# A two-layer hybrid decoder trunk: a changed order of work, u of the second layer handed over per 512 features, and a last normalisation without GpSimd

## The chip, the cores and the metric

The kernel runs on one core of one Trainium2 chip. The metric is the device time of one execution in microseconds; the figure of a kernel is the median of its runs. The core has five engines with a queue each: TensorE (PE in the profile, its weight loads PEld), VectorE (DVE), ScalarE (ACT), GpSimd (POOL) and SyncE (SP), which here issues almost all DMAs. An engine works through its queue in order, and waits at an instruction whose data is not there.

## The reference

Two layers, 256 rows of 1024 features, one batch. Each layer is:

```
mod = c @ w_ada + b_ada -> (shift, scale, gate)
u   = x * (1 + scale) + shift
h   = u @ w_in                      (one projection, columns split among groups)
o   = concat[DSA(4 heads), FoX(6 heads), NSA(6 heads)] * silu(g_path)
x   = LayerNorm(ALPHA * x + (1 + gate) * (o @ w_out)) * ln_g + ln_b
```

DSA is attention over the 64 best keys of each row, chosen by an indexer with 8 small heads. FoX is causal attention with a decay that is a running sum of log-sigmoids. NSA adds three branches: compressed keys, selected blocks and a window; at 256 rows the last two are both causal attention over all keys. The output is x after the second layer, in float32.

## The kernel before

**Products.** Each float32 operand of a projection is split in two: a rounded part (wh, uH, mH) and the rest (wl, uL, mL). A product is three matmuls in turn, rounded by rounded, rounded by rest, rest by rounded (`mm3`, L549 to L551). For a weight piece ACT makes wh (L516) and DVE wl (L534).

**Weights.** All weights are one stream of pieces of up to 128 x 1024 float32, 512 KB each, read in a fixed order (`stream_order`, L180) by SP into six raw buffers (L485). A raw buffer is free when DVE has made wl from it, or, for a piece of w_ada, when DVE has multiplied it with c and summed it up (`ada_gemv`, L583, one piece per 128 features and part). The order's parameters are `cord` (order of the four column chunks of layer 1), `tord0` and `tord1` (order of the 16 column tiles), `ada_at` and `adag_at` (behind which tile the pieces of w_ada come: the pair of a start and a step).

**Projections.** Four chunks, A to D, are projected with rows on the partitions: A holds the indexer, decay and NSA gates, B q and k of DSA, C keys of NSA, D queries of NSA; each also carries a part of the values. Layer 0 does all four chunks together, piece by piece. Layer 1 does them one after the other in the order `cord` (`proj_tok`, L1146); the first one takes rows 0 to 127 with its four pieces, then rows 128 to 255 with the same pieces. A unit is one piece of 256 features for one half of the rows, six matmuls. Then come 16 column tiles (`proj_col`, L1164): 0 and 1 are the compressed NSA keys and values, 2 to 7 keys and queries of the three FoX pairs (2 and 3 are pair 0, 4 and 5 pair 1, 6 and 7 pair 2), 8 to 15 the gate path, one per pair of heads (8 and 9 DSA, 10 to 12 NSA, 13 to 15 FoX).

**Attention.** Two heads make a pair (`attn_pair`, L713): scores in two PSUM banks (L722), row maximum on DVE (L677), exponential on ACT (L681), reciprocal sums on DVE (L667, L668), scaling on ACT (L694), transposes on PE (L704), copy on ACT (L708), product with the values on PE (L753), copy out of PSUM (L975). An NSA pair does this twice in one output bank and then waits for the compressed branch. The gate step (`out_gate`, L1123) takes one of four gate buffers, frees its PSUM bank once it has multiplied, waits for its head pair, and makes mH and mL.

**End of a layer.** The output projection is followed by `resid` (L1223): gate row times y (L1229), ALPHA x + that (L1232), statistics (L1234, L1245), then `rsqrt` (L1290): variance plus EPS on DVE (L1246), Ln and Exp on ACT (L1292, L1293), two ACT products that prepare a Newton step (L1294, L1295), and two DVE steps for it (L1297, L1298). After layer 0 x is normalised (L1263), PE transposes it (L1379, `next_u`), ACT makes u (L1389) and uH (L1403), and DVE uL (L1407, `u_block`), each for 512 features and 128 rows. The old layer's scale and shift go into the new layer's modulation; x itself gets them later (`affine`, L1420, four DVE operations L1430 per half of the rows). After layer 1 the rows 0 to 127 are normalised on ACT (L1281, `tail_first`) and get ln_g and ln_b on GpSimd (L1287, `tail_pool`); rows 128 to 255 get theirs on DVE (L1304, L1307, `tail`).

**What sets the order.** A planner (`Order`, L233) writes the queues out when the program is built. Each part of the work is a task that asks for an engine and states a cost, for buffers or PSUM banks, or for an event (`until`). The planner gives each engine the task that can start first, and among those that can start within 0.02 us of it (0.1 for a task of priority -2 or less) the one with the lowest priority number. The numbers stand in `PR` (L364), by layer where the name ends in 0 or 1: `nsa`, `dsa`, `fox` the pairs, `idx`, `topk`, `dec`, `cmp` the indexer, the selection, the decay and the compressed branch, `aff` the affine step, `ada` 6, the main stream 10. PSUM banks are given by class with a cap each: `acc` 4 of the 8 banks for projections, `o` 3 for outputs, `s` 2 for scores, `pt` 1 for transposes, `ms` 3. Events only shape the plan; on the chip an instruction waits for its data.

The event of the handover is set when both blocks of 512 features are there:

```
yield until(("ub", t, 0), ("ub", t, 1))     # next_u, L1381
od.set("u", 1, t)
...
yield until(("u", l, t), ("w", (c, l, q)))  # proj_tok, L1153
...
yield until(("u", 1, 0))                    # stream, L1435
```

Of the kernel before, what the change touches and what calls it, by code (L numbers as in the profile page):

```python
# [13 lines left out]
ALU = mybir.AluOpType  # L14
# [4 lines left out]
P = 128  # L19
# [341 lines left out]


RW = [6, 5]
PR = dict(zn='VV', upart=4, ul='VVVV', nrm='AAAA', cord='ABDC', t1q=0, cuts=(0, 512, 1024), oq=(0, 1, 2, 3), tord=(0, 1, 2, 3, 4, 5, 6, 7, 8, 9, 10, 11, 12, 13, 14, 15), gpp=(0, 1), res=-3.5, warm=10, tol=0.1, ada_at=(12, 0.25), adag_at=((0, 0.5), (11, 1)), ow=(512, 256), aff=0, tw=512, nact=((0, 0), (1, 0), (0, 1), (1, 1)), pro='', gp0=(0, 1), gp1=(0, 1), acc=4, s=2, pt=1, o=3, ms=3, side=8, topk=3, idx=2, dec=0.5, cmp=1.2, nsa=1.6, dsa=1.7, fox=1.8, gate=4, gate1=6, ada=6, main=10, ev=0, split=4, nahead=2, acc1=1.5, cmp1=3, dec0=1.45, nsa1=1.6, topk1=6, nsa0=1.3, dec1=0.5, idx1=0.3, tord1=(2, 3, 4, 5, 6, 7, 0, 1, 8, 9, 10, 11, 12, 13, 14, 15), dsa0=1.4, oq0=(1, 0, 2, 3), cmp0=1.2, fox1=1.5, dsa1=1.7, fox0=1.1, oq1=(1, 2, 3, 0), topk0=3, tord0=(0, 1, 2, 3, 4, 5, 6, 7, 8, 9, 10, 11, 12, 13, 14, 15), idx0=2, nrm1='AAAA', nrm0='AAAA', t1q0=0, t1q1=0)  # L364


@with_exitstack
def trunk(ctx: ExitStack, tc: tile.TileContext, xT, x, crow, wst, bcol, lnrow, pe_b, cst, cstb, out,
# [30 lines left out]
    def until(*names):  # L399
        return ("U", names)  # L400
# [14 lines left out]
    def small(shape, name, bufs=2, dt=F32, pool=None):  # L415
        return (pool or sm).tile(shape, dt, tag=name, name=nm(name), bufs=bufs)
# [350 lines left out]
    def layer(l, uH, uL):  # L767
# [378 lines left out]
        def proj_tok(c, t_outer=False):  # L1146
            n = len(CHUNKS[c])
            yield bank("acc", 2)
            accs = [ps(n) for _ in range(2)]
            units = [(t, q) for t in range(2) for q in range(4)] if t_outer else \  # L1150
                    [(t, q) for q in range(4) for t in range(2)]
            for t, q in units:
                yield until(("u", l, t), ("w", (c, l, q)))  # L1153
                yield ("P", rmm(n, 6))
                h, lo = piece((c, l, q), n)
                for k in (2 * q, 2 * q + 1):
                    ts = slice(t * P, (t + 1) * P)
                    mm3(accs[t], uH[:, k, ts], uL[:, k, ts], h[:, k % 2, :], lo[:, k % 2, :], k == 0, k == 7)
                if t == 1:
                    piece_done((c, l, q))  # L1160
                if q == 3:
                    od.spawn(EV[c](t, accs[t], "acc"), 0)
# [28 lines left out]
        if l == 0:  # L1191
            yield bank("abc", 8)
            accs = {c: [ps(len(CHUNKS[c])) for t in range(2)] for c in "ABCD"}
            for j in range(8):
                yield until(("uk", j))
                for grp in FIRST[j]:
                    key = (grp, l, j)
                    yield until(("w", key))
                    n = len(CHUNKS[grp[0]])
                    yield ("P", rmm(sum(len(CHUNKS[c]) for c in grp), 6))  # L1200
                    h, lo = ready[key]
                    for cc in grp:
                        cs = slice(0, n) if cc == grp[0] else slice(n, n + len(CHUNKS[cc]))
                        for t in range(2):
                            ts = slice(t * P, (t + 1) * P)
                            mm3(accs[cc][t], uH[:, j, ts], uL[:, j, ts], h[:, cs], lo[:, cs], j == 0, j == 7)
                    piece_done(key)
            od.set("u", 0, 0)
            od.set("u", 0, 1)
            for c in "ABCD":  # L1210
                for t in range(2):
                    od.spawn(EV[c](t, accs[c][t], "abc"), 0)
        else:
            for c in PR["cord"]:
                yield from proj_tok(c, t_outer=(c == PR["cord"][0]))
# [7 lines left out]
        def resid(t, o, w, acc):  # L1223
            yield until(("grow", l, o // 512))
            yield lock("t2k")
            xs = x_sb[:, t, o:o + w]
            yield ("V", cvec(w))
            tmp = buf("t2k", 512)[:, :w]
            V.tensor_tensor(tmp, acc, Gr[l][:, o:o + w], op=ALU.mult)  # L1229
            unbank("acc")  # L1230
            yield ("V", cvec(w, 2))
            V.scalar_tensor_tensor(xs, xs, ALPHA, tmp, op0=ALU.mult, op1=ALU.add)  # L1232
            for i in range(0, w, 256):
                V.bn_stats(stats[:, t, (o + i) // 256, :], xs[:, i:i + 256])  # L1234
            od.release("t2k")
            if o + w < D:
                return
            mv = small([P, 2], "mv", 2)
            ve = small([P, 1], "ve", 2)
            rs = small([P, 1], "rs", 2)  # L1240
            rm = small([P, 2], "rm", 2)
            tq = small([P, 1], "tq", 2)
            mu = mv[:, 0:1]
            yield ("V", 0.2)
            V.bn_aggr(mv, stats[:, t].rearrange("p n s -> p (n s)"))  # L1245
            V.tensor_scalar(ve, mv[:, 1:2], EPS, None, op0=ALU.add)  # L1246
            od.set("res", l, t)
            od.spawn(rsqrt(t, ve, rs, rm, tq), -3)
            if l + 1 < DEPTH:
                yield until(("rs", l, t))  # L1250
                if "A" in PR["zn"]:
                    nb = small([P, 1], "nb", 2)
                    yield ("V", 0.1)
                    V.scalar_tensor_tensor(nb, mu, -1.0, tq, op0=ALU.mult, op1=ALU.mult)
                od.spawn(next_u(l, t), -2)
                for q in range(2):
                    xs = x_sb[:, t, 512 * q:512 * q + 512]
                    if PR["zn"][q] == "A":
                        yield ("A", cact(512, 1))
                        A.activation(xs, xs, AF.Identity, bias=nb, scale=tq)  # L1260
                    else:
                        yield ("V", 0.12 + cfast(512))
                        V.tensor_scalar(xs, xs, mu, tq, op0=ALU.subtract, op1=ALU.mult)  # L1263
                    od.set("zn", t, q)
                od.spawn(affine(t), PR["aff"])
            elif t == 0:
                od.spawn(tail_first(mu, tq), 6)
            else:
                cuts = PR["cuts"]
                for i, (o0, o1) in enumerate(zip(cuts, cuts[1:])):  # L1270
                    od.spawn(tail(t, o0, o1, mu, tq, i), -2)

        def tail_first(mu, tq):
            nb = small([P, 1], "nb", 2)
            yield until(("rs", l, 0))
            yield ("V", 0.08)
            V.scalar_tensor_tensor(nb, mu, -1.0, tq, op0=ALU.mult, op1=ALU.mult)
            for h in range(2):
                xs = x_sb[:, 0, 512 * h:512 * h + 512]
                yield ("A", cact(512, 2))  # L1280
                A.activation(xs, xs, AF.Identity, bias=nb, scale=tq)  # L1281
                od.spawn(tail_pool(xs, h), 6)

        def tail_pool(xs, h):
            for i, op in enumerate((ALU.mult, ALU.add)):
                yield ("G", cpool(512))
                G.tensor_tensor(xs, xs, rows[l][i][:, 512 * h:512 * h + 512], op=op)  # L1287
            nc.sync.dma_start(out[:, 0, 512 * h:512 * h + 512], xs)

        def rsqrt(t, ve, rs, rm, tq):  # L1290
            yield ("A", 0.5)
            A.activation(rs, ve, AF.Ln)  # L1292
            A.activation(rs, rs, AF.Exp, scale=-0.5)  # L1293
            A.mul(rm[:, 0:1], rs, -0.5)  # L1294
            A.mul(rm[:, 1:2], rs, 1.5)  # L1295
            yield ("V", 0.54)
            V.scalar_tensor_tensor(tq, rs, rs, ve, op0=ALU.mult, op1=ALU.mult)  # L1297
            V.tensor_scalar(tq, tq, rm[:, 0:1], rm[:, 1:2], op0=ALU.mult, op1=ALU.add)  # L1298
            od.set("rs", l, t)

        def tail(t, o0, o1, mu, tq, i):
# [63 lines left out]
    def next_u(l, t):  # L1365
# [5 lines left out]
        for q in range(2):  # L1371
# [6 lines left out]
                j = 4 * q + i  # L1378
                T.transpose(pt[:, i, :], x_sb[:, t, P * j:P * j + P], ident)  # L1379
            od.spawn(u_block(q, pt, t), -2)  # L1380
        yield until(("ub", t, 0), ("ub", t, 1))  # L1381
        od.set("u", 1, t)

    def u_part(q, i, pt, u, t):
        j = 4 * q + i
# [9 lines left out]
    def u_block(q, pt, t):  # L1395
# [11 lines left out]
        (V if E == "V" else G).tensor_tensor(uL1[:, 4 * q:4 * q + 4, ts], u, uH1[:, 4 * q:4 * q + 4, ts].bitcast(F32), op=ALU.subtract)  # L1407
        od.release("t2k")
        od.set("ub", t, q)

    rows = {}

# [19 lines left out]

    def stream():
        yield from layer(0, uHs[0], uLs[0])
        yield until(("u", 1, 0))  # L1435
        yield from layer(1, uHs[1], uLs[1])

    u_tiles(0)
# [46 lines left out]
```

## Time and profile before

| | |
|---|---|
| median of 3 runs | 391.98 us (390.94 to 393.09) |
| the profiled execution | 391.34 us, of which its span 389.6 |
| mean granted clock of TensorE | 0.965 |
| PE busy | 352.2 us, 90% |
| DVE busy | 314.6 us, 81% |
| ACT busy | 252.6 us, 65% |
| POOL busy | 8.1 us, 2% |
| moved by DMA | 75.47 MB, mean 194 GB/s |

A row of a profile names engine, line, operation, the tiles it writes and reads, their shapes, and how many instructions were merged (x4). Times are microseconds; start times count from the span's start. L549 to L551, L516 and L534 are lines of helpers, so that the tiles tell what the row belongs to: wh,uH is an input projection, wh,mH an output projection. Tile b is any PSUM bank, q and f are attention operands, lnr rows of ln_g and ln_b, mv mean and variance. A busy PE may be one at half clock; the granted clock says so.

### The profile page before, as it was taken

What the parts mean: (1) busy time and instruction counts of PE and PEld (TensorE: products, weight loads), DVE (VectorE), ACT (ScalarE), POOL (GpSimd) and SP (SyncE); (2) the same over time, 40 slices, a digit from 0 to 9 for tenths busy, and PEclk for the clock granted to TensorE, in tenths of its full rate; (3) what the DMA queues carried; (4) which work ended last, traced back from release to release, by engine and by line L of the source; (5) the groups of instructions that cost most, each with busy time, mean ns of one, the idle gap of its engine ahead of it and who ended that gap; (6) DMA issues with size and microseconds to landing.
All of it is one profiled execution on the core that took longest, in us unless ns stands there. A gap on an engine that the chain in (4) does not pass through costs nothing.

```text
span 389.6 us, 6872 instructions
## 1 busy us (share of the span) xinstructions
PE 352.2 (90%) x2430; PEld 284.8 (73%) x2430; DVE 314.6 (81%) x766; ACT 252.6 (65%) x664; POOL 8.1 (2%) x14
## 2 busy tenths in 40 slices
PE   5899999799999998589977999999999999997990
PEld 1687788588886786377956768878888898864790
DVE  5798879998989998978899889999565688553766
ACT  3564458676996868773385656556998646987520
POOL 2000000000000000000000000000000000000014
PEclk9899999999999999979988999999999999998996
DMA  7999997638425658796644554563355695110002
GB/s 228 411 408 397 360 352 305 217 110 303 130 64 177 194 177 297 245 315 209 216 133 172 145 174 115 163 209 108 110 142 187 170 407 179 48 63 0 1 2 108
DMA packets 22074, 75.47 MB, mean 194 GB/s; under 512 B 2964, under 2 KB 3096, under 8 KB 21912
## 3 DMA queue, kind: packets, MB, share of 16 engines
q1 hardware_dynamic: 21752, 74.75, 57.1%
q8 instruction: 19, 0.31, 0.3%
q10 hardware_dynamic: 288, 0.29, 0.2%
q14 instruction: 15, 0.12, 0.1%
HBM read 73.98 MB, written 1.05 MB: 193 GB/s over the span
## 4 chain that ended last, share of the span: by engine, by line
PE 49%; DVE 26%; DMA 12%; ACT 8%; issue 4%; DVEq 0%; SPq 0%; ACTq 0%
DMA raw<-in_wst_dram 12%; PE b L549 11%; PE b L551 11%; PE b L550 10%; DVE wl L534 6%; PE b L722 4%; PE b L753 3%; PE b L704 3%; DVE raw L583 2%; DVE iacc L926 2%; DVE iacc L886 2%; ACT wh L516 2%; ACT p L694 2%; DVE m L925 2%; DVE roped L641 1%
## 5 line engine op out<-in xcount | busy, mean ns | idle before, releaser
L516 ACT CAST wh<-raw 128x1024 fp32r<-128x1024 f32 (+2 forms) x81 | 83.3, 1030 | 55.7 <-DMA raw<-in_wst_dram 28.4
L534 DVE TENSOR_TENSOR wl<-raw,wh 128x1024 fp32r<-128x1024 f32 (+2 forms) x81 | 96.2, 1193 | 13.7 <-ACT wh L516 12.9
L549 PE MATMUL b<-uH,wh 128*128 128x256 f32 x256 | 77.4, 302 | 0.0
L551 PE MATMUL b<-uH,wl 128*128 128x256 f32 x256 | 72.9, 285 | 0.2 <-DVE wl L534 0.2
L550 PE MATMUL b<-uL,wh 128*128 128x256 f32 x256 | 72.7, 284 | 0.0
L583 DVE SCALAR_TENSOR_TENSOR raw<-raw,cbc 128x1024 f32<-128x1024 f32 x48 | 58.0, 1218 | 4.3 <-DMA raw<-in_wst_dram 4.0
L549 PE MATMUL b<-wh,uH 128*128 128x512 f32 (+1 forms) x128 | 52.4, 410 | 3.0 <-ACT uH L1359 2.3
L551 PE MATMUL b<-wh,uL 128*128 128x512 f32 (+1 forms) x128 | 51.5, 402 | 3.3 <-DVE uL L1407 1.6
L549 PEld LDWEIGHTS b<-uH,wh 128*128 128x128 f32 x256 | 49.2, 192 | 2.4 <-issue 1.5
L550 PE MATMUL b<-wl,uH 128*128 128x512 f32 (+1 forms) x128 | 51.0, 398 | 0.0
L551 PEld LDWEIGHTS b<-uH,wl 128*128 128x128 f32 x256 | 49.2, 192 | 0.6 <-DVE wl L534 0.6
L550 PEld LDWEIGHTS b<-uL,wh 128*128 128x128 f32 x256 | 49.3, 193 | 0.1
L681 ACT ACTIVATE p<-b,nmx 128x128 f32<-128x128 f32 x88 | 36.3, 428 | 3.5 <-DVE nmx L677 3.4
L694 ACT ACTIVATE p<-p,rinv 128x128 f32<-128x128 f32 (+1 forms) x88 | 33.8, 451 | 2.8 <-DVE rinv L668 1.4
L551 PEld LDWEIGHTS b<-wh,uL 128*128 128x128 f32 x128 | 25.1, 196 | 10.6 <-DVE uL L1361 3.9
L704 PE MATMUL b<-cf,p 128*128 128x128 f32 x132 | 23.9, 290 | 9.4 <-ACT p L694 9.4
L549 PE MATMUL b<-wh,mH 128*128 128x256 f32 (+1 forms) x96 | 31.9, 332 | 0.5 <-ACT mH L1139 0.5
L551 PE MATMUL b<-wh,mL 128*128 128x256 f32 (+1 forms) x96 | 31.2, 325 | 0.5 <-DVE mL L1141 0.5
L549 PEld LDWEIGHTS b<-wh,uH 128*128 128x128 f32 x128 | 25.2, 197 | 8.8 <-ACT uH L1359 2.8
L550 PE MATMUL b<-wl,mH 128*128 128x256 f32 (+1 forms) x96 | 31.1, 324 | 0.0
L708 ACT COPY pT<-b 128x384 f32<-128x384 f32 x44 | 21.2, 484 | 11.6 <-PE b L704 11.1
L550 PEld LDWEIGHTS b<-wl,uH 128*128 128x128 f32 x128 | 24.9, 194 | 4.1
(174 smaller groups left out, 565.0 us busy)
## 6 DMA issues: line engine op xcount, KB each, us to landing
raw<-in_wst_dram SPq DMA_DIRECT2D x120, 512.0 KB, 4.6
raw<-in_wst_dram SPq DMA_DIRECT2D x7, 480.0 KB, 6.6
lnr<-in_lnrow_dram SPq DMA_DIRECT2D x4, 512.0 KB, 4.9
raw<-in_wst_dram SPq DMA_DIRECT2D x4, 448.0 KB, 4.1
xT_sb<-in_xT_dram SPq DMA_DIRECT2D x4, 256.0 KB, 6.6
x_sb<-in_x_dram SPq DMA_DIRECT2D x1, 1024.0 KB, 7.7
out_dram<-x_sb SPq DMA_DIRECT2D x3, 256.0 KB, 2.2
cf<-in_cst_dram SPq DMA_DIRECT2D x1, 384.0 KB
```

What stands on the lines that cost most here:

```text
L516: A.copy(h[:, :n], loaded[key])
L534: V.tensor_tensor(lo[:, :n], raw, h[:, :n].bitcast(F32), op=ALU.subtract)
L549: T.matmul(o, ah, bh, start=start, stop=False)
L550: T.matmul(o, ah, bl, start=False, stop=False)
L551: T.matmul(o, al, bh, start=False, stop=stop)
L583: V.scalar_tensor_tensor(w, w, 1.0, cbc, op0=ALU.mult, op1=ALU.mult, accum_out=mods[l][:, j, h:h + 1])
L681: A.activation(p_sb[:, P * t:P * t + P * (t + 1)], so[:, P * t:P * t + P * (t + 1)], AF.Exp, bias=nmx[:, t, a:a + 1], accum_out=st[:, t, a ...
L694: A.mul(blk, blk, r[:, t, a:a + 1])
L704: T.transpose(pt[:, i, :], p_sb[:, P * i:P * i + P], ident)
L708: A.copy(pT, pt.rearrange("p a b -> p (a b)"))
L722: T.matmul(sp[a][:, P * t:P * t + nk], qT[r, t * P:(t + 1) * P], kT[r, :nk], start=True, stop=False, skip_group_check=True)
L753: T.matmul(O[64 * a:64 * a + 64, P * kt:], vs(a, kt), outs[a][0][:, 256 * kt:256 + 128 * kt], start=(first and kt == 0), stop=(last and kt ...
```

## The change

Three things are changed. The planner's parameters are others: order of the chunks and of the column tiles, places of the w_ada pieces, priorities, the cap of class `acc` (4 to 5) and the order in which the output projection takes its pieces in layer 1 (`oq1`). The event u is set per half of the rows and block of 512 features, and the main stream of layer 1 may be planned from the first block on. The normalisation's root takes Ln of the variance with EPS as a bias tile, and the Newton step is written with -0.5 (var + EPS), so that the two ACT products fall away; the last rows 0 to 127 get ln_g and ln_b on DVE.

Of `PR`, only what differs is shown (old, new):

```
cord    'ABDC' -> 'DCAB'          ada_at  (12, 0.25) -> (10, 0.5)
adag_at ((0, 0.5), (11, 1)) -> ((0, 0.5), (8, 1))
aff     0 -> 0.49                 acc     4 -> 5
dec0    1.45 -> 0.28              nsa1    1.6 -> 5.08
topk1   6 -> 5.9                  idx1    0.3 -> 0.64
dsa0    1.4 -> 0.12               dsa1    1.7 -> 4.17
cmp0    1.2 -> 1.39               fox0    1.1 -> 1.48
fox1    1.5 -> 1.95               oq1     (1, 2, 3, 0) -> (1, 3, 2, 0)
tord0   (0, 1, 2, 3, ..., 15) -> (0, 1, 3, 4, 5, 6, 7, 8, 9, 10, 11, 12, 13, 2, 14, 15)
tord1   (2, 3, 4, 5, 6, 7, 0, 1, 8, 9, 10, 11, 12, 13, 14, 15)
     -> (2, 4, 6, 7, 0, 1, 8, 9, 5, 3, 14, 10, 12, 13, 11, 15)
```

```diff
+    eps = small([P, 1], "eps", 1)
+    V.memset(eps, EPS)
...
-                yield until(("u", l, t), ("w", (c, l, q)))
+                yield until(("u", l, t, q // 2), ("w", (c, l, q)))
...
-            V.tensor_scalar(ve, mv[:, 1:2], EPS, None, op0=ALU.add)
+            V.tensor_scalar(ve, mv[:, 1:2], EPS, -0.5, op0=ALU.add, op1=ALU.mult)
...
-                od.spawn(tail_pool(xs, h), 6)
+                od.spawn(tail_rows(xs, h), 6)
...
-                yield ("G", cpool(512))
-                G.tensor_tensor(xs, xs, rows[l][i][:, 512 * h:512 * h + 512], op=op)
+                yield ("V", cvec(512))
+                V.tensor_tensor(xs, xs, rows[l][i][:, 512 * h:512 * h + 512], op=op)
...
-            yield ("A", 0.5)
-            A.activation(rs, ve, AF.Ln)
+            yield ("A", 0.3)
+            A.activation(rs, mv[:, 1:2], AF.Ln, bias=eps)
             A.activation(rs, rs, AF.Exp, scale=-0.5)
-            A.mul(rm[:, 0:1], rs, -0.5)
-            A.mul(rm[:, 1:2], rs, 1.5)
-            yield ("V", 0.54)
-            V.scalar_tensor_tensor(tq, rs, rs, ve, op0=ALU.mult, op1=ALU.mult)
-            V.tensor_scalar(tq, tq, rm[:, 0:1], rm[:, 1:2], op0=ALU.mult, op1=ALU.add)
+            yield ("V", 0.3)
+            V.scalar_tensor_tensor(ve, rs, rs, ve, op0=ALU.mult, op1=ALU.mult)
+            V.scalar_tensor_tensor(tq, ve, 1.5, rs, op0=ALU.add, op1=ALU.mult)
...
-        yield until(("ub", t, 0), ("ub", t, 1))
-        od.set("u", 1, t)
...
         od.set("ub", t, q)
+        od.set("u", 1, t, q)
...
-        yield until(("u", 1, 0))
+        yield until(("u", 1, 0, 0))
```

More of the change, by code (lines that the diff above doesn't have):

```diff
@@ L363 @@
 RW = [6, 5]
-PR = dict(zn='VV', upart=4, ul='VVVV', nrm='AAAA', cord='ABDC', t1q=0, cuts=(0, 512, 1024), oq=(0, 1, 2, 3), tord=(0, 1, 2, 3, 4, 5, 6, 7, 8, 9, 10, 11, 12, 13, 14, 15), gpp=(0, 1), res=-3.5, warm=10, tol=0.1, ada_at=(12, 0.25), adag_at=((0, 0.5), (11, 1)), ow=(512, 256), aff=0, tw=512, nact=((0, 0), (1, 0), (0, 1), (1, 1)), pro='', gp0=(0, 1), gp1=(0, 1), acc=4, s=2, pt=1, o=3, ms=3, side=8, topk=3, idx=2, dec=0.5, cmp=1.2, nsa=1.6, dsa=1.7, fox=1.8, gate=4, gate1=6, ada=6, main=10, ev=0, split=4, nahead=2, acc1=1.5, cmp1=3, dec0=1.45, nsa1=1.6, topk1=6, nsa0=1.3, dec1=0.5, idx1=0.3, tord1=(2, 3, 4, 5, 6, 7, 0, 1, 8, 9, 10, 11, 12, 13, 14, 15), dsa0=1.4, oq0=(1, 0, 2, 3), cmp0=1.2, fox1=1.5, dsa1=1.7, fox0=1.1, oq1=(1, 2, 3, 0), topk0=3, tord0=(0, 1, 2, 3, 4, 5, 6, 7, 8, 9, 10, 11, 12, 13, 14, 15), idx0=2, nrm1='AAAA', nrm0='AAAA', t1q0=0, t1q1=0)
+PR = dict(zn='VV', upart=4, ul='VVVV', nrm='AAAA', cord='DCAB', t1q=0, cuts=(0, 512, 1024), oq=(0, 1, 2, 3), tord=(0, 1, 2, 3, 4, 5, 6, 7, 8, 9, 10, 11, 12, 13, 14, 15), gpp=(0, 1), res=-3.5, warm=10, tol=0.1, ada_at=(10, 0.5), adag_at=((0, 0.5), (8, 1)), ow=(512, 256), aff=0.49, tw=512, nact=((0, 0), (1, 0), (0, 1), (1, 1)), pro='', gp0=(0, 1), gp1=(0, 1), acc=5, s=2, pt=1, o=3, ms=3, side=8, topk=3, idx=2, dec=0.5, cmp=1.2, nsa=1.6, dsa=1.7, fox=1.8, gate=4, gate1=6, ada=6, main=10, ev=0, split=4, nahead=2, acc1=1.5, cmp1=3, dec0=0.28, nsa1=5.08, topk1=5.9, nsa0=1.3, dec1=0.5, idx1=0.64, tord1=(2, 4, 6, 7, 0, 1, 8, 9, 5, 3, 14, 10, 12, 13, 11, 15), dsa0=0.12, oq0=(1, 0, 2, 3), cmp0=1.39, fox1=1.95, dsa1=4.17, fox0=1.48, oq1=(1, 3, 2, 0), topk0=3, tord0=(0, 1, 3, 4, 5, 6, 7, 8, 9, 10, 11, 12, 13, 2, 14, 15), idx0=2, nrm1='AAAA', nrm0='AAAA', t1q0=0, t1q1=0)
 @with_exitstack
@@ L1207, in layer @@
                     piece_done(key)
-            od.set("u", 0, 0)
-            od.set("u", 0, 1)
             for c in "ABCD":
@@ L1240, in resid @@
             rs = small([P, 1], "rs", 2)
-            rm = small([P, 2], "rm", 2)
             tq = small([P, 1], "tq", 2)
@@ L1245, in resid @@
             V.bn_aggr(mv, stats[:, t].rearrange("p n s -> p (n s)"))
-            V.tensor_scalar(ve, mv[:, 1:2], EPS, None, op0=ALU.add)
+            V.tensor_scalar(ve, mv[:, 1:2], EPS, -0.5, op0=ALU.add, op1=ALU.mult)
             od.set("res", l, t)
-            od.spawn(rsqrt(t, ve, rs, rm, tq), -3)
+            od.spawn(rsqrt(t, mv, ve, rs, tq), -3)
             if l + 1 < DEPTH:
@@ L1281, in tail_first, with tail_rows, rsqrt @@
                 A.activation(xs, xs, AF.Identity, bias=nb, scale=tq)
-                od.spawn(tail_pool(xs, h), 6)
-        def tail_pool(xs, h):
+                od.spawn(tail_rows(xs, h), 6)
+        def tail_rows(xs, h):
             for i, op in enumerate((ALU.mult, ALU.add)):
-                yield ("G", cpool(512))
-                G.tensor_tensor(xs, xs, rows[l][i][:, 512 * h:512 * h + 512], op=op)
+                yield ("V", cvec(512))
+                V.tensor_tensor(xs, xs, rows[l][i][:, 512 * h:512 * h + 512], op=op)
             nc.sync.dma_start(out[:, 0, 512 * h:512 * h + 512], xs)
-        def rsqrt(t, ve, rs, rm, tq):
-            yield ("A", 0.5)
-            A.activation(rs, ve, AF.Ln)
+        def rsqrt(t, mv, ve, rs, tq):
+            yield ("A", 0.3)
+            A.activation(rs, mv[:, 1:2], AF.Ln, bias=eps)
             A.activation(rs, rs, AF.Exp, scale=-0.5)
-            A.mul(rm[:, 0:1], rs, -0.5)
-            A.mul(rm[:, 1:2], rs, 1.5)
-            yield ("V", 0.54)
-            V.scalar_tensor_tensor(tq, rs, rs, ve, op0=ALU.mult, op1=ALU.mult)
-            V.tensor_scalar(tq, tq, rm[:, 0:1], rm[:, 1:2], op0=ALU.mult, op1=ALU.add)
+            yield ("V", 0.3)
+            V.scalar_tensor_tensor(ve, rs, rs, ve, op0=ALU.mult, op1=ALU.mult)
+            V.scalar_tensor_tensor(tq, ve, 1.5, rs, op0=ALU.add, op1=ALU.mult)
             od.set("rs", l, t)
```

## The prediction

> **What bounds the kernel now.** I read the page first, then the table by stretches, then the order in time of PE, DVE and ACT where that table shows PE losing time. The profiled execution took 391.34 us (span 389.6), 0.64 below the median of the runs, 391.98. The terms are summed against 391.34 and the 0.64 added at the end. In the rows of the table by stretches the columns are the stretch, its length, busy time and count of PE, weight loads, DVE, ACT and POOL, then PE's granted clock, the DMA share and GB/s. Rows of the order in time begin with the start and the duration; a bracket at their end holds the idle time before and what ended it.
>
> ```profile
> 60.00:100.00 40.00, 36.12 (x325) 30.29 (x325) 37.30 (x111) 30.18 (x101) 0.00 (x0) 1.00 0.67 226
> 100.00:160.00 60.00, 58.02 (x475) 45.01 (x474) 55.03 (x165) 48.17 (x149) 0.00 (x0) 1.00 0.55 176
> 160.00:168.00 8.00, 2.35 (x12) 1.04 (x13) 6.97 (x15) 6.43 (x19) 0.00 (x0) 0.78 0.81 266
> 168.00:172.00 4.00, 4.00 (x22) 4.00 (x23) 4.00 (x5) 1.88 (x4) 0.00 (x0) 0.58 0.91 298
> 196.00:202.00 6.00, 3.64 (x25) 2.94 (x25) 5.56 (x13) 5.55 (x16) 0.00 (x0) 1.00 0.40 100
> 202.00:206.00 4.00, 3.84 (x13) 2.74 (x12) 3.77 (x6) 3.50 (x7) 0.00 (x0) 0.57 0.93 293
> 208.00:212.00 4.00, 1.92 (x11) 1.30 (x9) 3.86 (x12) 2.63 (x8) 0.00 (x0) 1.00 0.30 104
> 212.00:216.00 4.00, 4.00 (x13) 3.15 (x12) 3.48 (x8) 1.65 (x4) 0.00 (x0) 0.57 0.00 0
> 220.00:260.00 40.00, 40.00 (x209) 31.57 (x208) 37.76 (x97) 24.02 (x59) 0.00 (x0) 1.00 0.57 172
> 260.00:300.00 40.00, 39.08 (x326) 32.66 (x326) 29.16 (x87) 32.78 (x103) 0.00 (x0) 1.00 0.46 133
> 300.00:350.00 50.00, 50.00 (x454) 42.38 (x450) 33.38 (x85) 36.22 (x98) 0.00 (x0) 1.00 0.52 179
> 350.00:352.00 2.00, 0.57 (x5) 0.14 (x1) 1.75 (x7) 1.49 (x7) 0.00 (x0) 1.00 0.00 0
> 352.00:356.00 4.00, 3.94 (x15) 2.77 (x17) 0.83 (x4) 3.20 (x13) 0.00 (x0) 0.57 0.00 0
> 356.00:362.00 6.00, 4.25 (x26) 2.09 (x22) 1.31 (x4) 3.68 (x10) 0.00 (x0) 1.00 0.00 0
> ```
>
> From 220 to 350 PE has work in nearly every microsecond at full clock, so time is to be won only where it idles, or runs slowly after idling. Idle is length minus busy; slow time is busy times (1 - clock). Place A, the end of layer 0: 8.00 - 2.35 = 5.65 idle, then 4.00 x 0.42 = 1.7 slow, together 7.3 us. Place B1, the first half of the handover between layers: 2.36 + 0.16 idle and 3.84 x 0.43 = 1.65 slow, 4.2. Place B2, its second half: 2.08 idle and 4.00 x 0.43 = 1.7 slow, 3.8. Place C, the end of layer 1's attention: 1.43 + 0.06 + 1.75 idle and 3.94 x 0.43 = 1.7 slow, 4.9. Place D, 60 to 100: 3.9. Place E is the tail after the last matmul.
>
> **The handover (B1, B2).**
>
> ```profile
> 199.31 0.50 PE L549 MATMUL b<-wh,uH 128*128 128x512 f32 x1 [0.73 <-ACT uH L1403]
> ...
> 201.67 0.50 PE L551 MATMUL b<-wh,uL 128*128 128x512 f32 x1 [1.63 <-DVE uL L1407]
> ...
> 209.08 0.39 PE L550 MATMUL b<-wl,uH 128*128 128x512 f32 x1
> 209.31 0.40 PE L551 MATMUL b<-wh,uL 128*128 128x512 f32 x1
> 211.79 0.44 PE L655 MATMUL b<-cf,roped 128*128 128x128 f32 x2 [2.08 <-DVE roped L644]
> ...
> 212.54 0.63 PE L550 MATMUL b<-wl,uH 128*128 128x512 f32 x1
> 212.97 0.63 PE L551 MATMUL b<-wh,uL 128*128 128x512 f32 x1
> ```
>
> ```profile
> 206.91 0.69 DVE L1407 TENSOR_TENSOR uL<-t2k,uH 128x512 fp32r<-128x512 f32 x1 [0.67 <-ACT uH L1403]
> 207.52 2.74 DVE L1430 TENSOR_TENSOR x_sb<-x_sb,lnr 128x512 f32<-128x512 f32 x4
> ...
> 211.91 0.68 DVE L1407 TENSOR_TENSOR uL<-t2k,uH 128x512 fp32r<-128x512 f32 x1
> ```
>
> The order is written by the planner, but the chip waits for data. At 199.31 PE already starts on the first 512 features of rows 0 to 127, before the second half exists; so for these rows the new event takes nothing away. B1 is a wait for uL, late on DVE. I take 0 there; DVE's new order could give half of it back (2) or cost another such wait (1.6). For rows 128 to 255 it is different: the first half of uL is done at 206.91 + 0.69 = 207.60, yet no matmul uses it, because the plan puts these units after the second half (211.91), and transposes that wait for the rotated features stand in front. With the event per half, two of the four units of the first chunk can go at 209.54: 12 matmuls at 0.23 us (209.08 to 209.31), 2.7 us, more than the 2.08 of idle. The priority of the old layer's affine step, 0 to 0.49, takes its four operations (2.74 us) from in front of the rotation and the second uL, so that what is late next, that uL, should be there at about 212. The slow clock goes with the gap. B2: 3.8 saved. If the second uL stays late, all of it comes back: 0.
>
> Granted clock 0.57 follows a gap of 2.08 us here, and matmuls start 0.43 us apart against 0.23. The Trainium skill (TensorE: Matmul & The Clock Gate, Part 1) asks for an idle window of about 3.4 us before the clock halves; by that, a gap as short as this would cost its idle time alone, B2 would be worth 2.1 and the forecast below 1.7 us later. This trace differs, so the row decides.
>
> **The end of layer 0 (A).**
>
> ```profile
> 161.33 5.06 DMA raw<-in_wst_dram
> ```
>
> ```profile
> 164.24 1.05 ACT L516 CAST wh<-raw 128x1024 fp32r<-128x1024 f32 x1 [0.54 <-DMA raw<-in_wst_dram]
> ```
>
> ```profile
> L583 DVE SCALAR_TENSOR_TENSOR raw<-raw,cbc 128x1024 f32<-128x1024 f32 x17 | 20.3, 1216 | 0.0
> ```
>
> The second layer's 16 modulation pieces are read in a burst: 2 after column tile 12, 8 after tile 13, 6 after tile 14. They share SP's queue and the six raw buffers with the weights, and DVE needs 1.2 us for each (the last row, of the groups in 100 to 168, holds 17 such steps, a few of them for the gate). The chain of waits, whose row is the first, stands still for 5.06 us for a weight behind the burst, and ACT's cast of it waits for the DMA too. The new order reads 2, 4, 4, 4 and 2 after the 11th to 15th tile, and puts fox pair 0's key tile behind the 13th, so that one pair's attention is left as cover. Tiles 11 to 13 then wait behind up to four pieces each; attention covers that, since PE is at 58.02 of 60 there. DVE sets the limit: it idles 60 - 55.03 = 5.0 us in 100 to 160 and 1.0 in 160 to 168, so the same work can end at most 6.0 earlier. Nothing is saved if the pieces fall between attention steps that DVE has to do first; I take 3.5, above the middle, for two reasons seen here: the pieces are DVE's lowest task, and the burst is the direct cause. Bounds 6.0 and -1.
>
> **Layer 1's order and its end (C).** The chunks come as D, C, A, B, so indexer and top-k start two chunks later, out of the stretch where DVE is at 37.76 of 40 and into one with 29.16 of 40. PE is full in both, so I count 0. Key tiles of the compressed branch come two tiles earlier, and fox and DSA rank above NSA.
>
> ```profile
> 326.54 0.91 ACT L975 COPY osb<-b 128x256 f32<-128x256 f32 x3
> ```
>
> ```profile
> 344.38 0.49 PE L722 MATMUL b<-q,q 64*128 64x128 f32 x4
> ...
> 347.58 0.49 PE L722 MATMUL b<-q,q 64*128 64x128 f32 x4
> ...
> 361.99 0.50 PE L549 MATMUL b<-wh,mH 128*128 128x512 f32 x1 [0.46 <-ACT mH L1139]
> ```
>
> Now the three NSA pairs hold all three output banks until 326.54, and the five other pairs run behind them, DSA last. Two DSA pairs start 3.2 us apart, and from the last pair's scores to its output projection pass 14.4 us, 4.9 of them lost. Some last pair always shows such a chain; finishing the compressed branch earlier leaves tile work to lie beside it. I take 1.0, bounds 4 and -4. D keeps its 3.9 (bounds 2 either way), since the rotations that PE awaits there are not changed.
>
> **The tail (E).**
>
> ```profile
> 376.53 0.22 DVE L1297 SCALAR_TENSOR_TENSOR tq<-rs,ve 128x1 f32<-128x1 f32 x1 [0.51 <-ACT rs L1293]
> ...
> 377.70 0.42 DVE L1232 SCALAR_TENSOR_TENSOR x_sb<-x_sb,t2k 128x256 f32<-128x256 f32 x1
> 378.16 0.43 DVE L1234 BATCH_NORM_STATS2 bn<-x_sb 128x6 f32<-128x256 f32 x1
> 379.95 0.42 DVE L1229 TENSOR_TENSOR t2k<-b,row 128x256 f32<-128x256 f32 x1 [1.37 <-PE b L551]
> 380.41 0.65 DVE L1232 SCALAR_TENSOR_TENSOR x_sb<-x_sb,t2k 128x256 f32<-128x256 f32 x1
> ...
> 381.93 0.81 DVE L1304 SCALAR_TENSOR_TENSOR x_sb<-x_sb,mv,lnr 128x512 f32<-128x512 f32 x1
> 382.66 1.21 DVE L1297 SCALAR_TENSOR_TENSOR tq<-rs,ve 128x1 f32<-128x1 f32 x1
> ```
>
> ```profile
> 378.26 5.59 POOL L1287 TENSOR_TENSOR x_sb<-x_sb,lnr 128x512 f32<-128x512 f32 x4 [375.20 <-ACT x_sb L1281]
> ```
>
> The 1-element step takes 1.21 instead of 0.22, and ends when POOL does (378.26 + 5.59 = 383.85); a residual step takes 0.65 instead of 0.42. Without POOL these 1.0 and 0.2 go. Against it, DVE gets four row steps, by the affine row 2.74 / 4 = 0.69 each. Two fit into its idle 1.37; the planner leaves small gaps between the steps of one task, where a low task slips in, so I count one on the chain, 0.7. The shorter reciprocal root drops two ACT steps beside the chain, and DVE's own row step at 381.93, which stands ahead of the 1-element step in its queue, covers what starting Ln earlier saves: 0. POOL's work leaves its queue, and SP's two output issues come no later than now, ahead of the last one. E: 1.2 - 0.7 = 0.5 saved, bounds 1.9 (every row step hidden, the root's steps worth something) and -0.9 (three slip in). The new constant is one small DVE step under the first loads: 0.
>
> **Sum.** 3.8 + 3.5 + 1.0 + 0.5 = 8.8. 391.34 - 8.8 = 382.5, and with 0.64, 383.2 us.
>
> **The rivals.** *Only the gaps that the rows fix are won* (0.24): in layer 0 DVE, 92% busy from 100 to 160, does the pieces no earlier, and C stays. B2 and E give 4.3: 387.7. For it: DVE's share. Against: PE's gap lies just behind the burst.
>
> *The gap returns* (0.08): PE fills 209.5 to 212 and then waits for the second uL, and A and C give nothing: 391.98 - 0.5 = 391.5. For it: DVE has 3.86 of 4.00 in that stretch. Against: 2.74 of those are affine steps that now rank lower.
>
> *Slower: the gates hold PSUM* (0.16). The accumulator class may hold 5 of 8 banks, not 4. Four gated tiles keep the four gate buffers until their heads are done, and DSA's two gates still come first; the next ones then sit in banks, and attention is left with 3, where one round wants two for scores, one for output and one for transposes. Rounds that now start 3.2 us apart then run singly, at 14.4 each. One such round costs 11.2: 391.98 - (3.8 + 3.5 + 0.5) + 11.2 = 395.4. It decides as soon as one pair more than now is open when the fifth gate waits. For it: DSA is late now with its mask long made. Against: units of the output projection can lie beside the round.
>
> **How the numbers follow.** My forecast has 0.52. Half a percent, 1.96 us, is about what a measurement of this kernel tells from no change: faster is below 390.0, slower above 393.9. Faster: 0.52 + 0.24 = 0.76; same 0.08; slower 0.16. For the range, all terms at their good ends would be 6.0 + 3.8 + 2 + 4 + 1.9 + 2 = 19.7, down to 372.3; I stop at 375, since not all hold together, and go up to 391, past the second case, which leaves out about 0.2.
>
> **What would show it.** Right: no gap of over 1 us in PE between the first chunk's two row blocks, and a clock of 1.00 through it; PE's idle between the last column tiles of layer 0 halved; the 1-element step near 0.22 in the tail and POOL without work there. Wrong: PE waiting longer for softmax results in the last 40 us before the output projection, new idle in the now full stretch 220 to 350, or modulation pieces still on DVE when PE runs dry.

## The result and the profile after

The changed kernel takes 375.08 us (median of 4 runs, 374.36 to 377.19), the kernel before 392.53 in the runs beside it (390.94 to 394.65). The ratio is 0.956, with a 95% interval of 0.950 to 0.962: 17.4 us less, twice the 8.8 of the sum. The median is inside the range by 0.08 us; two of the four runs lie below it. The profiled execution took 374.79 us, span 373.0; the mean clock went from 0.965 to 0.978.

First the table by stretches of the kernel after, cut where its stages end: layer 0's attention and last column tiles, its output projection, the handover, the other chunks, column tiles with attention, the output projection in two parts, the tail. Columns as in the prediction.

```profile
145.00:168.35 23.35, 18.18 (x138) 14.99 (x135) 20.56 (x45) 18.73 (x54) 0.00 (x0) 0.93 0.84 270
168.35:194.30 25.95, 25.45 (x163) 21.88 (x162) 23.31 (x46) 13.64 (x22) 0.00 (x0) 1.00 0.65 226
194.30:216.00 21.70, 18.46 (x95) 15.38 (x94) 21.02 (x37) 16.83 (x39) 0.00 (x0) 1.00 0.61 194
216.00:248.20 32.20, 32.20 (x154) 24.56 (x152) 24.99 (x57) 18.66 (x42) 0.00 (x0) 1.00 0.64 199
248.20:338.20 90.00, 90.00 (x800) 76.16 (x802) 73.59 (x216) 75.58 (x224) 0.00 (x0) 1.00 0.46 146
338.20:345.00 6.80, 6.80 (x41) 4.83 (x41) 3.63 (x8) 4.26 (x10) 0.00 (x0) 1.00 0.44 154
345.00:363.50 18.50, 18.50 (x127) 17.10 (x126) 14.02 (x28) 6.47 (x8) 0.00 (x0) 1.00 0.01 1
363.50:373.00 9.50, 0.01 (x1) 0.00 (x0) 5.94 (x14) 0.50 (x2) 0.00 (x0) 0.68 0.30 110
```

Three things are to be seen. From 206 on PE has no idle time until its last matmul, and its clock is 1.00 from 194 to there: place C is gone altogether. The handover still has 21.70 - 18.46 = 3.2 us of idle, but no slow stretch. The end of layer 0 still loses 23.35 - 18.18 = 5.2 us of idle and 18.18 x 0.07 = 1.3 slow.

Where the time went is clearest from five landmarks in PE's order in time, here in us from the span's start (profiles, one execution each):

| kernel | layer 0's column tiles end | layer 1's chunks begin | chunks end | output projection ends | span |
|---|---|---|---|---|---|
| before | 173.1 | 199.3 | 259.0 | 379.9 | 389.6 |
| after | 168.3 | 194.3 | 248.2 | 363.5 | 373.0 |

The stage before the chunks is 5.0 us shorter, the chunks 5.8 (59.7 to 53.9), the rest up to the last matmul 5.6 (120.9 to 115.3), the tail 0.2. In that third stage the kernel before loses 0.9 us idle from 259 to 338, and 3.25 idle and 1.45 slow from 338 to 362 by these rows of it:

```profile
259.00:338.00 79.00, 78.08 (x698) 68.13 (x697) 57.39 (x153) 59.05 (x166) 0.00 (x0) 1.00 0.52 169
338.00:362.00 24.00, 20.75 (x130) 12.91 (x128) 10.04 (x32) 19.24 (x63) 0.00 (x0) 0.93 0.14 45
```

0.9 + 3.25 + 1.45 = 5.6: as near as these rows tell, the gain of that stage is the time that PE lost there.

### The profile page after: what moved, and what is told of

The parts are those of the page before. It is cut to its first block, busy times and chain, and to the rows that moved or that the text cites. A ratio compares the mean times of both kernels' runs of the same rounds, so it can differ in the third digit from the quotient of the medians.

```text
span 373.0 us, 6834 instructions
## 1 busy us (share of the span) xinstructions
PE 344.9 (92%) x2430; PEld 282.7 (76%) x2430; DVE 314.8 (84%) x771; ACT 251.7 (67%) x656; POOL 2.5 (1%) x10
## 4 chain that ended last, share of the span: by engine, by line
PE 70%; DMA 12%; DVE 11%; ACT 4%; issue 2%; SPq 0%; DVEq 0%; ACTq 0%
PE b L551 16%; PE b L553 15%; PE b L552 15%; DMA raw<-in_wst_dram 12%; PE b L724 5%; PE b L755 5%; PE b L706 4%; DVE raw L585 2%; DVE wl L536 2%; ACT wh L518 2%; PE b L657 2%; PE b L734 2%; PE b L908 2%; ACT t2k L1384 1%; PE b L627 1%
## 5 line engine op out<-in xcount | busy, mean ns | idle before, releaser
L536 DVE TENSOR_TENSOR wl<-raw,wh 128x1024 fp32r<-128x1024 f32 (+2 forms) x81 | 96.0, 1193 | 14.4 <-ACT wh L518 13.4
L553 PE MATMUL b<-wh,uL 128*128 128x512 f32 (+1 forms) x128 | 50.6, 395 | 2.7 <-DVE uL L1358 1.5
L551 PE MATMUL b<-wh,uH 128*128 128x512 f32 (+1 forms) x128 | 51.0, 399 | 2.0 <-ACT uH L1356 2.0
L552 PE MATMUL b<-wl,uH 128*128 128x512 f32 (+1 forms) x128 | 50.2, 392 | 0.3 <-DVE wl L536 0.3
L679 DVE TENSOR_REDUCE nmx<-b 128x1 f32<-128x128 f32 x88 | 25.4, 347 | 0.3 <-PE b L734 0.2
```

The source lines that it names most:

```text
L536: V.tensor_tensor(lo[:, :n], raw, h[:, :n].bitcast(F32), op=ALU.subtract)
L551: T.matmul(o, ah, bh, start=start, stop=False)
L552: T.matmul(o, ah, bl, start=False, stop=False)
L553: T.matmul(o, al, bh, start=False, stop=stop)
L679: V.tensor_reduce(nmx[:, t, a:a + 1], so[:, P * t:P * t + P * (t + 1)], axis=AX.X, op=ALU.max, negate=True)
```

## The experiments

Each kernel ran beside the kernel before (whose median lay between 392.4 and 392.9). A ratio is to the kernel before, with its 95% interval.

**The three parts alone.** The theory was that order, handover and normalisation add up, the order first. The rival was that the order pays only through the handover.

*Handover alone.* The events `u` per half in the kernel before, as in the diff above.

> The kernel before with one part of the change: the event u per half of the rows and 512 features. If the finer handover is worth what the prediction put on it, the time falls by 3 to 4 us (ratio 0.990 to 0.992), and PE's 2.08 us gap between the two row blocks of the first chunk is gone. If the event only shapes the plan and the gap is set by data on DVE and ACT, the time stays within 1 us (ratio 0.997 to 1.003) and a gap of about 2 us stays before the rotated features are transposed.

386.97 us, ratio 0.986 (0.981 to 0.992): 5.5 us. PE's order in time where it waits, then two stretches after the waits:

```profile
200.19 0.50 PE L549 MATMUL b<-wh,uH 128*128 128x512 f32 x1 [0.73 <-ACT uH L1399]
202.54 0.50 PE L551 MATMUL b<-wh,uL 128*128 128x512 f32 x1 [1.62 <-DVE uL L1403]
211.39 0.38 PE L655 MATMUL b<-cf,roped 128*128 128x128 f32 x2
...
212.98 0.50 PE L551 MATMUL b<-wh,uL 128*128 128x512 f32 x1 [0.23 <-DVE uL L1403]
```

```profile
202.50:206.50 4.00, 3.96 (x19) 3.29 (x20) 3.67 (x7) 3.50 (x8) 0.00 (x0) 1.00 0.97 275
...
213.00:217.00 4.00, 4.00 (x18) 3.29 (x19) 4.00 (x6) 2.93 (x6) 0.00 (x0) 1.00 0.16 31
```

This is the mechanism of the prediction: the first half's units fill the gap, the transposes at 211.39 no longer wait (2.08 before), the second uL costs 0.23, and the clock stays at 1.00. B1's waits, 0.73 and 1.62, stand as they were. PE's queue says the same: 36 matmuls of the first chunk stand ahead of these transposes, where the kernel before has 24, so the six matmuls each of two units have moved up.

*Normalisation alone.* Root and row steps of the change in the kernel before.

> The kernel before with the shorter root and the last row steps on VectorE. Theory: the tail after the last matmul falls by 0.2 to 0.5 us, and the two roots between the layers give another 0.2, so the ratio is 0.998 to 1.000; the 1-element step is near 0.22 us and three row steps stand in the chain. Rival, that taking GpSimd out is what counts: 1.2 us or more off the tail, ratio 0.997 or less.

396.82 us, ratio 1.010 (1.005 to 1.015): slower, which neither expected. PE waits 3.62 us for x of the rows 128 to 255, where the kernel before waited 0.16:

```profile
208.87 1.11 PE L1376 MATMUL b<-cf,x_sb 128*128 128x128 f32 x4 [3.62 <-DVE x_sb L1262]
```

PE's queue differs from the kernel before in one place only:

```diff
+MATMUL b<-cf,x_sb 128x128 x4
 (six matmuls of layer 0's output projection)
-MATMUL b<-cf,x_sb 128x128 x4
```

These four are not the transposes that wait for 3.62 us. They are the first ones, of rows 0 to 127, which now stand six matmuls earlier. The queues of ACT and DVE differ too. On DVE a `wl` step that stands behind the first half of x of the rows 128 to 255 in the kernel before now stands ahead of the root's two steps for these rows:

```profile
206.20 1.23 DVE L536 TENSOR_TENSOR wl<-raw,wh 128x1024 fp32r<-128x1024 f32 x1
207.35 0.21 DVE L1294 SCALAR_TENSOR_TENSOR ve<-rs,ve 128x1 f32<-128x1 f32 x1
...
208.27 0.54 DVE L1262 TENSOR_SCALAR x_sb<-x_sb,mv,tq 128x512 f32<-128x512 f32 x1
```

The planner was told a cheaper root (0.3 and 0.3 for 0.5 and 0.54) and wrote all three queues by it. Which of the changed places makes x late was not tried one by one. To test the costs as a whole, the same instructions with the old ones:

```diff
-            yield ("A", 0.3)
+            yield ("A", 0.5)
             A.activation(rs, mv[:, 1:2], AF.Ln, bias=eps)
...
-            yield ("V", 0.3)
+            yield ("V", 0.54)
```

> The shorter root and the row steps on VectorE, without the rest of the change, as in the second run, but the planner is told the old costs of the root (0.5 on ACT, 0.54 on DVE). PE's queue is then the same as before, where the second run had the transposes of rows 128 to 255 six matmuls earlier. If those transposes, waiting for x behind DVE, are why the second run was 1% slower, the time is now 0 to 0.5 us below the kernel before (ratio 0.998 to 1.000). If the instructions themselves cost it, it is again about 1% slower.

391.77 us, ratio 0.998 (0.995 to 1.001). PE's queue is the old one, and the loss is gone. No cost of the instructions shows; a number given to the planner cost 1%. The expectation names the wrong transposes: those that had stood six matmuls earlier are of rows 0 to 127.

*Order alone.* `PR` of the change in the kernel before.

> The kernel before with the changed planner parameters alone. Theory: the order of work carries most of the gain, 12 to 14 of the 16.6 us (ratio 0.965 to 0.970). Rival, that the order pays only because the main stream of layer 1 may start from the first half: 6 us or less (ratio 0.985 or more).

378.08 us, ratio 0.963 (0.958 to 0.968): 14.4 us. The rival falls.

*Handover and normalisation taken back, one at a time, from the changed kernel.* The first with `until(("u", l, t), ...)` and the whole-row event again, the second with the old root and GpSimd.

> The changed kernel with u handed over whole again, 1024 features at a time. If the handover is worth 3 to 4 us beside the new order, the time rises by that, to about 378.5. If the event only shapes the plan, it stays within 1 us of the changed kernel, 374 to 376.

381.03 us, 5.9 above the changed kernel: its runs (380.87 to 383.83) and the changed kernel's do not overlap. So the handover is worth 5.9 us here, more than expected.

> The changed kernel with the old root and the rows 0 to 127 on GpSimd: the order and the handover alone. If the normalisation is worth its 0.2 us in the tail and no more, the time is 374.5 to 376. If the second run's loss belongs to the normalisation, this kernel is 3 to 4 us faster than the changed one, near 371.5.

374.85 us (373.43 to 375.09), ratio 0.954 (0.950 to 0.958): no difference that these runs can tell from the changed kernel. The tail, from the last matmul to the end, is 9.6 with GpSimd and 9.5 without.

The theory that the three parts add up does not hold. These are the medians side by side:

| parts of the change in the kernel | us |
|---|---|
| none | 392.4 to 392.9 |
| handover | 386.97 |
| normalisation | 396.82 |
| order | 378.08 |
| order and normalisation | 381.03 |
| order and handover | 374.85 |
| all three | 375.08 |

The new normalisation costs 4.4 us alone and 3.0 beside the new order (378.08 to 381.03; the runs do not overlap), and nothing that shows once the handover is there too. The handover is worth 5.5 us alone, 3.2 beside the new order with the old normalisation (378.08 to 374.85), and 5.9 with the new one: there it also takes away what the normalisation costs. Whether the planner's costs are the reason beside the new order too was not tested.

**The order by layers.**

```
 layer 0 alone: ada_at, tord0, dec0, dsa0, cmp0, fox0, aff of the change
 layer 1 alone: cord, adag_at, nsa1, topk1, idx1, fox1, dsa1, tord1, oq1 of the change (acc stays 4)
```

> The kernel before with the parameters that concern layer 0 and the affine step alone (ada_at, tord0, dec0, dsa0, cmp0, fox0, aff). Theory: layer 1 starts about 5 us earlier, as in the changed kernel (199.3 to 194.3), and nothing else moves: ratio 0.987. Rival, that DVE bounds layer 0: layer 1 starts less than 2 us earlier, ratio 0.995 or more.

387.11 us, ratio 0.988 (0.982 to 0.995): 5.3 us. Its landmarks: column tiles end at 168.4, chunks begin at 195.4, and from there on all is as before, within 1.3 us.

> The kernel before with the parameters of layer 1 alone (cord, adag_at, nsa1, topk1, idx1, fox1, dsa1, tord1, oq1; the accumulator cap stays 4). Theory: the last attention pairs get tile work beside them, so that the 4.9 us lost before the output projection go, and some idle in the middle: 5 to 8 us, ratio 0.980 to 0.987. Rival, that the cap of five accumulators is needed for it: 2 us or less.

384.81 us, ratio 0.978 (0.971 to 0.985): 8.1 us. From the end of the chunks to the last matmul it takes 115.3 us (257.1 to 372.5), as the changed kernel does, with a cap of 4: the cap of 5 is not needed for it. Layer 0's 5.3 and layer 1's 8.1 come near to the 14.4 of the whole order.

**Why the end of layer 1 lost time.** The theory: the NSA pairs hold the three output banks until the compressed branch is done. The rival: priorities. In the kernel before only the order of layer 1's tiles changes:

```diff
-tord1=(2, 3, 4, 5, 6, 7, 0, 1, 8, ..., 15)
+tord1=(0, 1, 2, 3, 4, 5, 6, 7, 8, ..., 15)
```

> The kernel before with only the two tiles of the compressed branch moved from the 7th and 8th place to the 1st and 2nd in layer 1 (tord1 = 0 to 15). If the three NSA pairs that hold all output banks until the compressed branch is done are what puts five pairs at the end, the banks come free some 15 us or more earlier than 326.5, FoX pairs start then, and 3 to 6 us are saved (ratio 0.985 to 0.992). If the priorities are what counts, the FoX and DSA pairs still start at about 326 or the time stays within 1 us.

389.27 us, ratio 0.991 (0.987 to 0.995): 3.2 to 3.6 us by the medians. ACT's first copy out of an output bank, PE's first FoX scores, and all that PE waited for from 262 to the last matmul:

```profile
306.47 0.38 ACT L975 COPY osb<-b 128x256 f32<-128x256 f32 x1
```

```profile
307.77 0.49 PE L722 MATMUL b<-f,f 64*128 64x128 f32 x4
```

```profile
PE b L655 <- DVE roped L644: 0.9, 2, 0.7
```

The banks are free 20 us earlier than 326.54, FoX starts at once, and PE waits 0.9 us where the kernel before waits 4.2. The stage from the end of the chunks to the last matmul takes 115.3 us (261.8 to 377.0) here too: these two tiles alone bring it to where the changed kernel has it, and the priorities are not needed for that. The 5.6 is a high figure, though. The profile of the kernel before has the longest of six such stages with the old order of tiles (119.7 to 120.9, mean 120.2), so that the mean gain is 4.9; the seven profiles with these tiles earlier all take 115.3 or 115.4. The 4.9 lies within the ratio's interval, which is 2.0 to 5.1 us. Up to the end of the chunks the queues of PE and DVE are the same as before, so their later end here (261.8 for 259.0) is a difference between executions. Now the reverse, on the changed kernel:

```diff
-tord1=(2, 4, 6, 7, 0, 1, 8, 9, 5, 3, 14, 10, 12, 13, 11, 15)
+tord1=(2, 4, 6, 7, 8, 9, 5, 3, 0, 1, 14, 10, 12, 13, 11, 15)
```

> The changed kernel with only the two tiles of the compressed branch moved back in layer 1, from the 5th and 6th place to the 9th and 10th. If they are the cause, the output banks come free 10 us or more later than 303.5, PE idles again before the output projection, and 3 to 6 us of the gain are lost. If priorities and the cap are the cause, the time stays within 1 us of the changed kernel.

383.03 us, 8.0 above the changed kernel, more than expected. First the kernel after, then this one: the first copies out of output banks.

```profile
303.52 0.65 ACT L977 COPY osb<-b 128x256 f32<-128x256 f32 x2
```

```profile
320.82 0.92 ACT L977 COPY osb<-b 128x256 f32<-128x256 f32 x3
```

The banks come free 17 us later, PE idles before the output projection again (it is busy 8.63 of 10 us from 330 on, 4.48 of 5 from 340), and the stage takes 121.0 us. What the other 2 us are was not tried.

**The end of layer 0.** Only the places of the modulation pieces, in the kernel before:

```diff
-ada_at=(12, 0.25)
+ada_at=(10, 0.5)
```

> The kernel before with only the places of the second layer's modulation pieces changed in layer 0 (two tiles earlier, spread out). If the burst is what starves PE at the end of layer 0, this gives 4 us or more of the 6 that the whole order of layer 0 gives there, and layer 1 starts at about 195 to 196. If the pair kept back as cover is what counts, it gives less than 2 us.

389.32 us over ten runs, 388.85 without the slowest (392.25), which the ratio leaves out: 0.991 (0.987 to 0.994), 3.7 us. Layer 1 starts at 198.9, not at 195 to 196 as expected; in this profile layer 0's chunks already end 2.4 us later (60.3 for 57.8). By the stage from the last matmul of layer 0's chunks to the last of its output projection it is 4.4: that takes 137.5 us here, 140.4 to 143.5 (mean 142.0) in six profiles with the old order of layer 0, and 135.4 to 137.1 (mean 136.3) in six with the new one. So, as far as one profile tells, the burst is most of the 5.7. Two stretches of it, where the kernel before was busy for 8.47 and 4.35 of 10:

```profile
150.00:160.00 10.00, 9.28 (x72) 6.56 (x70) 8.90 (x25) 8.68 (x27) 0.00 (x0) 1.00 0.74 229
160.00:170.00 10.00, 7.34 (x47) 6.29 (x46) 8.15 (x16) 7.04 (x22) 0.00 (x0) 0.83 0.90 306
```

Then the changed kernel with the pieces earlier still, `ada_at=(8, 0.5)`:

> The changed kernel with those pieces another two tiles earlier (from the 9th tile). If the pieces still starve PE at 145 to 160, some of the 6.4 us lost there go, 1 to 3 us. If DVE is the limit now, the time stays within 1 us of the changed kernel or rises, as attention steps come later.

384.79 us, 9.7 above the changed kernel; a rise was expected of one theory, but not this one. From 127 to 143 PE gets no projection of a column tile at all; what ACT and PE waited for from 100 to 170:

```profile
ACT wh L518 <- DMA raw<-in_wst_dram: 5.6, 5, 3.3
...
PE b L551 <- ACT wh L518: 3.0, 2, 2.2
PE b L553 <- DVE wl L536: 2.7, 3, 1.2
```

Layer 1 begins at 204.4 instead of 194.3. A cause that fits is that the pieces now stand in front of tiles 10 to 13 on SP's queue, so that PE has too little to do beside attention; it is argued, not shown. All of PE's waits for weights in these rows fall behind 150. From 127 to 143 PE idles for 2.7 us, and what it waits for there is mostly attention (2.0 us for its transposed scores). Of the three places that ran, the middle one is the best.

## Why the prediction was right, and where its size was off

**Direction and places** were right. That the median also lies inside the range is luck: it does so by 0.08 us, less than the runs differ. Of the four terms the handover came out at 0.8 to 1.6 times its forecast, by what stands beside it, the end of layer 0 at 1.5 times, layer 1's order at eight times, and the tail at nothing that the runs tell.

**The handover**: forecast 3.8, measured 5.5 alone, 3.2 beside the new order, and 5.9 beside order and normalisation. The mechanism is shown by the first run. In the changed kernel itself it looks different from what was forecast:

```profile
194.34 0.37 PE L551 MATMUL b<-wh,uH 128*128 128x448 f32 x1
...
195.68 0.47 PE L553 MATMUL b<-wh,uL 128*128 128x448 f32 x1 [0.77 <-DVE uL L1402]
...
204.13 0.55 PE L657 MATMUL b<-cf,roped 128*128 128x128 f32 x3 [2.02 <-DVE roped L646]
```

A gap of 2.02 us before the rotated features is still there. Even the first half of u for the rows 128 to 255 is late here (DVE begins its uL at 203.99), so nothing can fill it. It is not the new order that brings this gap. With the same order and handover and the old normalisation, DVE begins that uL at 201.13, twelve matmuls of the rows 128 to 255 run from 202.40 on, and PE does not wait for the rotated features:

```profile
202.40 0.36 PE L549 MATMUL b<-wh,uH 128*128 128x448 f32 x1
...
205.03 0.55 PE L655 MATMUL b<-cf,roped 128*128 128x128 f32 x3
```

So "no gap of over 1 us between the first chunk's two row blocks" holds there and not in the changed kernel, and both take the same time: as a sign of the gain it was a poor one. The clock of 1.00 was right. Without the handover the same order is worse: with the old normalisation PE waits 4.0 us for x between 188 and 222 and its clock falls to 0.51 and 0.64; with the new one it waits 2.6 for x and 2.9 for rotated features, at 0.60 and 0.55.

**The end of layer 0**: forecast 3.5 with a bound of 6.0 from DVE's idle time, measured 5.3. The cause was named rightly, and most of it is the burst. The sign did not come: PE's idle time from 145 to the last column tile was not halved, it fell from 7.2 to 5.2 us. The bound was nearly reached: in the changed kernel DVE is busy for 19.55 of 20 us from 160 to 180, where it was for 16.79. The lost time on which the term was based came from the shortest of six executions of that stage, so that it was too low by some 1.5 us.

**Layer 1's order**: forecast 1.0, measured 8.1. This is the step that failed: "Some last pair always shows such a chain ... I take 1.0". The row that held the answer was quoted, output banks taken until 326.54, and the two earlier tiles were counted, with the right effect, that "tile work" would "lie beside it"; but the end was priced as if a chain of 14.4 us must stay bare. In the changed kernel the last DSA pair's scores start at 330.14 and its output is copied at 343.66, 13.5 us later (13.1 in the kernel before, 347.58 to 360.67), and PE works through all of it:

```profile
330.14 0.49 PE L724 MATMUL b<-q,q 64*128 64x128 f32 x4
```

```profile
343.66 0.37 ACT L977 COPY osb<-b 128x256 f32<-128x256 f32 x1 [1.68 <-PE b L755]
```

Column tiles run on until 338.2 beside it and out-projection units after that. A chain's length says nothing of its cost while other work is in the queue; tiles used up between 294 and 326, when no new pair began, were the work that was missing at the end. The tile order accounts for 4.9 to 5.6 of the 8.1. The other part had been put at nothing: "PE is full in both, so I count 0", of the chunks' order. From the last matmul of layer 0's output projection to the end of layer 1's chunks, the run with layer 1's order takes 57.2 us (52.3 for the chunks, a wait for x of 4.0 ahead of them), and four profiles with the old one take 60.8 to 61.2. No run changes `cord` alone, so which parameter does this stays open, and so do the single priorities.

**The tail**: forecast 0.5, measured 0.2, and nothing that the runs can tell. The saving came as forecast: the 1-element step is back to 0.21 us, the residual step to 0.42. The price did not: one row step was counted, and three slip in front of the last block, so that it starts 1.3 us after the last matmul (0.03 in the kernel before):

```profile
362.94 2.00 DVE L1286 TENSOR_TENSOR x_sb<-x_sb,lnr 128x512 f32<-128x512 f32 x3
364.86 0.42 DVE L1229 TENSOR_TENSOR t2k<-b,row 128x256 f32<-128x256 f32 x1
...
367.25 0.21 DVE L1294 SCALAR_TENSOR_TENSOR ve<-rs,ve 128x1 f32<-128x1 f32 x1
```

**The rivals.** That only the gaps of the rows are won, that the gap returns, and that gates hold PSUM did not come: after 206 PE waits for nothing, and the gap of 2.02 us that is left is not followed by a slow clock. That a cheaper root could cost 1% was not among them. It does not show in the changed kernel, since the handover is there; without it the new normalisation costs 3.0 us beside the same order.

## What to carry to other kernels

Ask of each scarce buffer who holds it, and what the holder waits for: two tiles read a little earlier gave back all that PE lost in the last stage, 4.9 us in the mean of the profiles and 3.2 to 3.6 by the medians, since they let three banks go. Price an exposed chain by the other work that will be in the queue beside it, not by its length, and look for the place where that work was spent. Where queues are written by a planner, a cost given to it is part of the kernel: compare the queues of all engines in two versions before the instructions are blamed. Measure a part both alone and beside the others: here one part took away what another cost.

## What the runs showed of the hardware

The clock after a gap is less regular than the prediction took it to be. Three profiles have the same PE queue up to the same wait (1.62 or 1.63 us for uL) at the start of the handover. The kernel before was then at half clock for 3.4 us, the handover alone not at all, and the kernel with the two tiles first for 6.8 us, but at full clock after its later gap of 2.10 us.

The traces' records of the granted clock show why. Leaving out the first 10 and the last 8 us of a span, every stretch at half clock lasts 3.41 or 6.83 us, and within a trace all of them lie on one grid of 3.41 us. Here is PE in some cells of that grid, for the kernel before, the handover alone, and the kernel with the two tiles first; the clock is the third column from the end:

```profile
198.68:202.09 3.41, 1.15 (x4) 0.68 (x5) 3.23 (x8) 2.96 (x11) 0.00 (x0) 1.00 0.69 175
202.09:205.51 3.42, 3.26 (x11) 2.25 (x10) 3.19 (x6) 2.92 (x6) 0.00 (x0) 0.50 0.94 282
...
208.92:212.33 3.41, 1.32 (x8) 0.79 (x7) 3.31 (x11) 2.06 (x7) 0.00 (x0) 1.00 0.13 50
212.33:215.74 3.41, 3.41 (x10) 2.65 (x9) 3.15 (x7) 1.43 (x4) 0.00 (x0) 0.50 0.00 0
```

```profile
200.46:203.88 3.42, 1.80 (x8) 1.14 (x8) 3.05 (x8) 2.98 (x10) 0.00 (x0) 1.00 0.70 224
203.88:207.29 3.41, 3.41 (x19) 2.80 (x18) 3.23 (x5) 2.88 (x7) 0.00 (x0) 1.00 0.96 309
```

```profile
201.63:205.04 3.41, 1.71 (x6) 0.97 (x6) 3.04 (x8) 2.97 (x11) 0.00 (x0) 1.00 0.70 189
205.04:208.46 3.42, 2.80 (x9) 2.22 (x9) 3.42 (x5) 2.93 (x6) 0.00 (x0) 0.50 0.97 323
208.46:211.87 3.41, 3.41 (x9) 2.55 (x9) 2.70 (x5) 0.77 (x2) 0.00 (x0) 0.50 0.92 325
211.87:215.28 3.41, 2.06 (x11) 1.38 (x9) 1.59 (x7) 2.64 (x8) 0.00 (x0) 1.00 0.03 13
215.28:218.70 3.42, 2.67 (x13) 2.24 (x14) 3.28 (x9) 1.26 (x4) 0.00 (x0) 1.00 0.00 0
```

What goes with the slow clock is how busy PE was in the cell ahead, in these rows 1.15, 1.32 and 1.71 of 3.41 us. In all fourteen traces, with the same ends left out, a full-clock cell in which PE was busy for under 42% (as the profile models its busy time) was followed by half clock each time (29 of 29), one over 62.5% never (0 of 1331), and one between in 16 of 36. The grid lies elsewhere in each execution, so the same gap costs the 1.7 us or not by where a cell happens to cut it: for one gap they are a chance, not a price. The Trainium skill (TensorE: Matmul & The Clock Gate, Part 1) says that the activity window runs freely and does not start with the work, which fits this; that a window has to be idle, as it asks, does not show here, since one that was busy for 1.15 of 3.41 us was followed by half clock.

A 1-element step on DVE took 1.21 us in every profile in which GpSimd worked on its row steps beside it, and 0.21 or 0.22 in those without. The Trainium skill (SBUF — State Buffer, Who interferes with whom) has the two engines share one pair of ports as an exclusive lock, held for a whole instruction; a step of GpSimd takes 1.3 to 1.7 us here, and the slow step ends with GpSimd's last one (383.87 and 383.85 in the kernel before), which agrees.
